# One transfer per convolution row and an earlier reload in a hybrid SSD / S5 / Conformer trunk

## The chip, the cores and the metric

The program runs on one core of one Trainium2 chip. Its time is device time in microseconds (us): 1638.1 us median of 3 runs (1636.99 to 1638.96). The engines are TensorE (PE: matrix products, with a weight load of its own, PEld), VectorE (DVE), ScalarE (ACT), GpSimd (POOL) and SyncE (SP), which here issues nearly all transfers (DMA) from one queue. Each engine runs its instructions in the order in which they stand. PE multiplies 128 x 128 weights with up to 512 columns; its results land in PSUM banks.

## The reference, cut to what matters

512 prompt tokens and 8 x 8 sample tokens (576 columns) of width 1024 pass through two layers. The change is in layer 0:

```python
xn = rms_norm(x)
proj = xn @ w_in_ab                         # z | x,B,C | dt | u
xbc = silu(causal_depthwise_conv(xbc, w=4)) # 2048 channels
cum = cumsum(dt * a)                        # per chunk of 128 tokens, 16 heads
y_diag = (scores * exp(cum_i - cum_j) * dt) @ x      # inside a chunk, causal
y_off  = C @ h_in * exp(cum)                          # from the state before the chunk
h = h * exp(cum_end) + B^T (exp(cum_end - cum) dt x)  # state, chunk to chunk
ya = group_rms_norm((y + d * x) * silu(z))  # 4 groups of 4 heads
yb = s5(u); yb = yb * sigmoid(yb @ w_glu)   # S5 mixer with its GLU
x  = x + concat(ya, yb) @ w_out
```

Then a squared-ReLU MLP; layer 1 is a Conformer convolution module and another MLP; a final norm. Outputs are the activations and the final states of both groups.

## The kernel before

Activations lie with channels on the 128 partitions and the 576 tokens along the row (`NT` = 576, `NP` = 512 prompt tokens, then 64 sample tokens). A product (`mm`, line 232) takes one block of 128 output channels: `load` (line 217) brings 128 x 1024 weights into `raw` (one 512 KB transfer), ACT makes the rounded part `hi`, DVE the rest `lo`, and PE adds hi x act-high, hi x act-low and lo x act-high for 8 blocks of inputs and 2 halves of the tokens: 48 matmuls of 288 columns. Inputs are split in the same way (`split`, `split_scaled`: high part on ACT, low part on DVE).

Layer 0 runs in `mixer0` (line 1061): the S5 input products with the scan, then 24 products of `w_in` (4 groups x [B, C, two of x, two of z]), 8 of `w_glu`, 8 + 8 of `w_out`. Beside them runs the side work of three kinds:
- `s5_y`: eight S5 outputs, the last step of S5; each result `y` goes to a DRAM tensor `yg`.
- `a_conv` (line 767), 16 times, once for each 128 channels of x, B, C. A product's result is copied to `pj` and stored in `prd` (`stash`). `a_conv` loads it to `xb`, multiplies with the norm, does four taps in `cvo` (ACT the first, DVE three 600-wide steps, L784), tanh on ACT (L786), the last step on DVE (L787), and stores to `xsd`. Prompt columns and the 8 x 8 sample columns go in separate transfers, since the sample tokens lie 11 apart in the tile (3 state columns before each 8): L773/L774 load, L788/L789 store. `xb` and `cvo` share one ring of three buffers (tag "cv").
- `a_group` (line 879), four SSD groups, two of them at a time: reload of the rows (`xs`, L889), transposes (`tr`), scores (`scr`), sample state (`h`, `yoff`), then five chunks, each with `sg` (a broadcast load of `cumd`, L943), `yps`, `st` and the state `hst` that goes from chunk to chunk.

`reload` (line 1153) brings the input of the next product back from DRAM: after the input projection `yg` (into `rl`, split to `yh` and `yl`), after the GLU `ybd` (split to `ybh` and `ybl`). The `rl` tiles rotate over three buffers that `pj` uses too.

The order on each engine is set by a scheduler from priorities: code written earlier goes first, and `hp(n)` moves a piece n places ahead. Weights stand 3000 ahead (`HP`), evacuations 149 (`HPE`), the side work 54 (`HPS`); `reload` stands at its place in the code. The side work is called after each product by `side`.

Of the kernel before, what the change touches and what calls it, by code (L numbers as in the profile page):

```python
# [8 lines left out]
F32 = mybir.dt.float32  # L9
F32R = mybir.dt.float32r  # L10
AF = mybir.ActivationFunctionType
ALU = mybir.AluOpType
# [3 lines left out]
NT = 576  # L16
NP = 512
# [121 lines left out]
def h2(t):  # L139
    return t.rearrange("p (h n) -> p h n", h=2)  # L140


class Build:
# [31 lines left out]
    GL = 7  # L175
    X2 = 8
    HPS = 54

    def X(self, name):
        return self.xp.tile([128, NT], F32, tag="X", name=name)  # L180

    def bank(self, name, tag="sd"):
        return self.pd.tile([128, 512], F32, tag=tag, name=name)
# [583 lines left out]
    def a_conv(self, m, rB):  # L767

        nc, q = self.nc, self.q1
        xb = q.tile([128, 603], F32, tag="cv", name="xb", bufs=3)  # L770
        s8 = lambda t, k, n: t[:, 515:603].rearrange("p (b j) -> p b j", b=8)[:, :, k:k + n]
        nc.gpsimd.memset(xb[:, 0:3], 0.0)
        nc.sync.dma_start(xb[:, 3:515], self.prd[m][:, 0:NP])  # L773
        nc.sync.dma_start(s8(xb, 3, 8), self.prd[m][:, NP:].rearrange("p (b j) -> p b j", b=8))  # L774
        nc.scalar.activation(s8(xb, 0, 3), self.aco[:, m, 0:8, :], AF.Copy)
        nc.vector.tensor_tensor(xb[:, 3:515], xb[:, 3:515], rB[:, 0:NP], op=ALU.mult)
        nc.vector.tensor_tensor(s8(xb, 3, 8), s8(xb, 3, 8), rB[:, NP:].rearrange("p (b j) -> p b j", b=8), op=ALU.mult)
        nc.scalar.activation(self.aco[:, m, 8, :], xb[:, 512:515], AF.Copy)
        nc.scalar.activation(self.aco[:, m, 0:8, :], s8(xb, 8, 3), AF.Copy)

        o = q.tile([128, 603], F32, tag="cv", name="cvo", bufs=3)
        nc.scalar.activation(o[:, 0:600], xb[:, 0:600], AF.Identity, scale=self.half("acw", m), bias=self.half("acb", m))  # L782
        for k in range(1, 4):
            nc.vector.scalar_tensor_tensor(o[:, 0:600], xb[:, k:k + 600], self.half("acw", 16 * k + m), o[:, 0:600],  # L784
                                           op0=ALU.mult, op1=ALU.add)
        nc.scalar.activation(xb[:, 0:600], o[:, 0:600], AF.Tanh)  # L786
        nc.vector.scalar_tensor_tensor(o[:, 0:600], xb[:, 0:600], 1.0, o[:, 0:600], op0=ALU.add, op1=ALU.mult)  # L787
        nc.sync.dma_start(self.xsd[m][:, 0:NP], o[:, 0:NP])  # L788
        nc.sync.dma_start(self.xsd[m][:, NP:].rearrange("p (b j) -> p b j", b=8), s8(o, 0, 8))  # L789

    def a_dt_in(self, ps, rB):
        df = self.qs.tile([128, NT], F32, tag="dtf", name="dtf", bufs=1)
        with self.hp(self.HPE):
            self.nc.vector.tensor_tensor(h2(df)[:32], ps[:32], h2(rB)[:32], op=ALU.mult)
        return df

    def a_dt(self, df):

        nc, q = self.nc, self.q1
# [9 lines left out]
        b = self.bank("dtT")  # L809
        for c in range(5):  # L810
            p = 128 if c < 4 else 64
# [3 lines left out]
        for p, c in ((128, slice(0, 4)), (64, slice(4, 5))):  # L815
            k = c.stop - c.start
# [4 lines left out]
        a, e, d, s, z = w(), w(), w(), w(), w()  # L821
# [23 lines left out]
        b = self.bank("cum")  # L845
# [24 lines left out]
        ch = self.qs.tile([128, NT], F32, tag="u3", name="ch", bufs=self.U3)  # L870
        nc.scalar.activation(ch[:16, 0:NP], c0[:16], AF.Copy)
        nc.scalar.activation(ch[:16, NP:], c1[:16, 0:64], AF.Copy)
        nc.sync.dma_start(self.cumd, ch[:16])
        ec = self.u3("ec", NT)
        nc.scalar.activation(ec[:16, 0:NT], ch[:16], AF.Exp)
        nc.sync.dma_start(self.ecd, ec[:16, 0:NT])
# [1 line left out]
    def a_group(self, g, q, X, bank, rB0):  # L878

        nc = self.nc  # L880
        u = str(g % 2)
        k2 = lambda name, *sh: q.tile([128, *sh], F32, tag="sg" + u, name=name, bufs=3)
        k1 = lambda name, *sh: q.tile([128, *sh], F32, tag="k1" + u, name=name, bufs=5)
        hg = slice(4 * g, 4 * g + 4)
        hp = lambda t: t.rearrange("p (h d) -> p h d", h=4)

# [19 lines left out]
        for c in range(5):  # L906
            tok = slice(c * 128, min(c * 128 + 128, NT))
            o = b0[:, tok] if c < 4 else b1[:64, 0:64]
# [12 lines left out]
        b = bank("yoff")  # L921
        for i in range(2):
            h0 = q.tile([128, 4, 256], F32, tag="h0" + u, name="h0", bufs=1)
            nc.sync.dma_start(h0, self.I["ass"][g, :, 4 * i:4 * i + 4, :])
            for j in range(2):
                for s in range(4):
                    t0 = 32 * i + 8 * s
# [5 lines left out]
        for c in range(5):  # L933
            T, t0 = (128, c * 128) if c < 4 else (64, NP)
            tok = slice(t0, t0 + T)
            per = lambda t: t[:T, c, hg].unsqueeze(2).broadcast_to([T, 4, 64])
            xd, xw = k1("xd", 256), k1("xw", 256)
            nc.vector.tensor_tensor(hp(xd[:T]), hp(xt[:T, c]), per(self.dt), op=ALU.mult)
            for e in range(4):
                nc.scalar.activation(xw[:T, e * 64:(e + 1) * 64], xt[:T, c, e * 64:(e + 1) * 64], AF.Copy,  # L940
                                     scale=self.dw[:T, c, 4 * g + e:4 * g + e + 1])
            sg = k2("sg", 4, 128)
            nc.sync.dma_start(sg[:, :, :T], bass.AP(tensor=self.cumd.tensor, offset=self.cumd.offset + 4 * g * NT + t0,  # L943
                                                    ap=[[0, 128], [NT, 4], [1, T]]))
            for e in range(4):

                nc.scalar.activation(sg[:T, e, :T], sg[:T, e, :T], AF.Relu, scale=-1.0, bias=self.cum[:T, c, 4 * g + e:4 * g + e + 1])
            nc.scalar.activation(sg[:T, :, :T], sg[:T, :, :T], AF.Exp, scale=-1.0)
            nc.vector.tensor_tensor(sg[:T, :, :T], sg[:T, :, :T], sc[:T, tok].unsqueeze(1).broadcast_to([T, 4, T]), op=ALU.mult)
            ps = bank("yps")  # L950
            for e in range(4):
                nc.tensor.matmul(ps[64 * (e % 2):64 * (e % 2) + 64, (e // 2) * 128:(e // 2) * 128 + T],  # L952
                                 xd[:T, e * 64:(e + 1) * 64], sg[:T, e, :T], start=True, stop=True)
            if 0 < c < 4:
                t, eb = k1("yt", 2, 128), k1("eb", 2, 128)
                for i in range(2):
                    nc.sync.dma_start(eb[64 * i:64 * i + 64],
                                      bass.AP(tensor=self.ecd.tensor, offset=self.ecd.offset + (4 * g + i) * NT + t0,
                                              ap=[[0, 64], [2 * NT, 2], [1, 128]]))
                for j in range(2):  # L960
                    nc.tensor.matmul(ps[:, 256 + j * 128:384 + j * 128], Hs[:, j * 128:(j + 1) * 128], Cg[:, tok], start=True, stop=True)
                nc.vector.tensor_tensor(t, ps[:, 256:512].rearrange("p (j t) -> p j t", j=2), eb, op=ALU.mult)
                for j in range(2):
                    nc.vector.tensor_tensor(ya[j][:, tok], ps[:, j * 128:(j + 1) * 128], t[:, j], op=ALU.add)
            else:
                for j in range(2):
                    if c < 4:
                        nc.scalar.activation(ya[j][:, tok], ps[:, j * 128:j * 128 + T], AF.Copy)
                    else:
                        nc.vector.tensor_tensor(ya[j][:, tok], ps[:, j * 128:j * 128 + T], yos[:, j], op=ALU.add)  # L970
            if c == 4:
                nc.sync.dma_start(self.btd[g], bt[:64, 4])
                nc.sync.dma_start(self.xwd[g], xw[:64])
            if c < 4:
                b = bank("st")
                nc.tensor.matmul(b[:, 0:256], bt[:, c], xw, start=True, stop=True)
                if c == 0:
                    nc.scalar.activation(Hs, b[:, 0:256], AF.Copy)
                else:
                    nc.vector.tensor_tensor(hp(Hs), hp(Hs), self.cd[:, c, hg].unsqueeze(2).broadcast_to([128, 4, 64]), op=ALU.mult)  # L980
                    nc.vector.tensor_tensor(Hs, Hs, b[:, 0:256], op=ALU.add)
                if c == 3:
                    nc.sync.dma_start(self.O["o_assm"][g, :, 8, :], Hs)
            yield
# [13 lines left out]
        rB = self.bcast_tok(r, "rg", X, bank)  # L998
# [62 lines left out]
    def mixer0(self):  # L1061
        nc, I = self.nc, self.I
        with self.tc.tile_pool(name="q1", bufs=5) as self.q1, ExitStack() as inner:
            self.qs = inner.enter_context(self.tc.tile_pool(name="qs", bufs=2))
            x = []
            for k in range(8):
                t = self.X("xi%d" % k)
# [4 lines left out]
            _, rB = self.rms(x, "rB0")  # L1072
# [6 lines left out]
            for m in range(8):  # L1079
                ps = self.mm(I["w_in"][m], act)  # L1080
                if m < 2:
                    t = self.t("ur", "t")
# [29 lines left out]
            def side(na):  # L1112
# [5 lines left out]
                for _ in range(na):  # L1118
                    with self.hp(self.HPS):
                        if conv:  # L1120
# [33 lines left out]
            def reload(d, f):  # L1154
                out = []
                for k in range(len(d)):
                    t = self.t("rl", "t")
                    nc.sync.dma_start(t, d[k])
                    out.append(f(k, t))
                return out  # L1160

            act = reload(self.yg, lambda k, t: self.split(t, "y", self.B))
# [4 lines left out]
            for m in range(8):  # L1167
                ps = self.mm(I["w_out"][8 + m], act)
                t = self.t("xr", "t")
# [9 lines left out]
            for m in range(8):  # L1179
                t = self.X("x%d" % m)  # L1180
# [249 lines left out]
```

## Time and profile before

| | |
|---|---|
| median of 3 runs | 1638.1 us |
| the profiled execution, its span | 1634.0 us, 1632.2 us |
| PE busy | 1574.1 us (96%) |
| DVE busy, ACT busy | 1056.4 us (65%), 642.3 us (39%) |
| PE's mean granted clock | 0.975 |
| DMA packets, of them under 512 bytes | 185,907, 92,560 |
| mean DMA rate | 135 GB/s |

The profile comes from one execution. "PEclk" or granted clock is the mean share of PE's full clock (2.4 GHz) in a stretch; the lower level is half of it. An idle time is put down to the one that ended it. A transfer "lands" when its data is there and its semaphore is raised. Everything that the change touches stands between 100 and 500 us; the busy times and waits are read in stretches of it below.

### The profile page before, as it was taken

The numbers are of one execution on the slowest core, as the hardware profiler recorded it, in microseconds if no ns is written. First come the engines' busy times: TensorE is split into PE (matmuls) and PEld (weight loads), VectorE is DVE, ScalarE is ACT, GpSimd is POOL, SyncE is SP. The second block draws the span as 40 slices with busy tenths as digits, with TensorE's granted clock in tenths as the row PEclk, the third lists the DMA queues.
The fourth block names the chain that finished last, engine by engine and source line by source line (L and its number), as shares of the span: only waits on it lengthen the run. The fifth ranks groups of instructions, "written<-read, shape, count | busy, mean of one in ns | idle before, by whom it ended". The sixth has DMA issues, their size and how long they took to land.

```text
span 1632.2 us, 28709 instructions
## 1 busy us (share of the span) xinstructions
PE 1574.1 (96%) x11765; PEld 1549.3 (95%) x11765; DVE 1056.4 (65%) x1757; ACT 642.3 (39%) x1084; POOL 4.3 (0%) x42
## 2 busy tenths in 40 slices
PE   7999998989899999999999999997899999999997
PEld 6999998889899999999999999996899999999996
DVE  7968986688865547677744457997554444434466
ACT  4243377775643343332222243332443322222243
POOL 0000000000000000000000000000000000000000
PEclk9999999979899999999999999998899999999998
DMA  5644587988863234454322235541122222222233
GB/s 189 184 120 142 158 226 220 298 251 241 241 229 136 78 96 160 156 135 105 101 79 78 91 133 154 167 136 45 42 88 79 78 91 78 79 90 78 91 118 135
DMA packets 185907, 220.18 MB, mean 135 GB/s; under 512 B 92560, under 2 KB 128400, under 8 KB 185776
## 3 DMA queue, kind: packets, MB, share of 16 engines
q1 hardware_dynamic: 182112, 217.03, 44.3%
q8 instruction: 92, 1.51, 0.4%
q10 hardware_dynamic: 3664, 1.32, 0.3%
q14 instruction: 39, 0.32, 0.1%
HBM read 184.10 MB, written 34.20 MB: 134 GB/s over the span
## 4 chain that ended last, share of the span: by engine, by line
PE 84%; DVE 8%; DMA 5%; issue 1%; ACT 1%; SPq 0%; ACTq 0%; DVEq 0%
PE mm L239 76%; PE pc L1326 2%; DVE acc L1389 1%; DVE lo L225 1%; PE yoff L928 1%; DMA by<-s5bc 1%; PE bc L323 1%; DMA eb<-ecd 1%; DMA xsd<-cvo 1%; PE s5s L613 1%; PE kt L572 1%; PE tsum L293 1%; DVE u L589 1%; PE mu L1301 0%; PE yps L952 0%
## 5 line engine op out<-in xcount | busy, mean ns | idle before, releaser
L224 ACT ACTIVATE hi<-raw 128x1024 fp32r<-128x1024 f32 x217 | 229.7, 1059 | 729.4 <-PE mm L239 633.3
L239 PE MATMUL mm<-fxh,hi 128*128 128x288 f32 x1920 | 417.6, 299 | 14.6 <-ACT hi L224 10.4
L225 DVE TENSOR_TENSOR lo<-raw,hi 128x1024 fp32r<-128x1024 f32 x217 | 264.8, 1221 | 248.0 <-ACT hi L224 243.4
L239 PE MATMUL mm<-fxh,lo 128*128 128x288 f32 x1920 | 415.4, 298 | 0.1
L239 PE MATMUL mm<-fxl,hi 128*128 128x288 f32 x1920 | 414.9, 297 | 0.0
L239 PEld LDWEIGHTS mm<-fxh,hi 128*128 128x128 f32 x1920 | 311.5, 190 | 16.3 <-ACT hi L224 11.3
L239 PEld LDWEIGHTS mm<-fxh,lo 128*128 128x128 f32 x1920 | 311.0, 190 | 1.0 <-DVE lo L225 0.7
L239 PEld LDWEIGHTS mm<-fxl,hi 128*128 128x128 f32 x1920 | 311.1, 190 | 0.5 <-issue 0.2
L239 PE MATMUL mm<-gh,lo 128*128 128x288 f32 x1024 | 229.1, 295 | 1.1 <-DVE lo L225 1.1
L239 PE MATMUL mm<-gh,hi 128*128 128x288 f32 x1024 | 229.6, 295 | 0.0
L239 PE MATMUL mm<-gl,hi 128*128 128x288 f32 x1024 | 229.2, 295 | 0.0
L239 PEld LDWEIGHTS mm<-gh,lo 128*128 128x128 f32 x1024 | 167.9, 188 | 1.5 <-DVE lo L225 1.5
L239 PEld LDWEIGHTS mm<-gl,hi 128*128 128x128 f32 x1024 | 168.3, 188 | 0.0
L239 PEld LDWEIGHTS mm<-gh,hi 128*128 128x128 f32 x1024 | 167.9, 188 | 0.0
L363 DVE TENSOR_TENSOR fft<-mm,r2B 128x576 f32<-128x576 f32 x56 | 42.3, 756 | 116.3 <-PE mm L239 116.3
L1389 DVE SCALAR_TENSOR_TENSOR acc<-hb,vec,acc 128x512 f32<-128x512 f32 x110 | 82.2, 747 | 1.5
L357 DVE TENSOR_TENSOR gl<-ffr,gh 128x576 fp32r<-128x576 f32 x64 | 48.4, 757 | 1.9
L356 DVE TENSOR_TENSOR ffr<-ffr 128x576 f32<-128x576 f32 x64 | 48.5, 757 | 1.6
L355 ACT ACTIVATE gh<-ffr 128x576 fp32r<-128x576 f32 x64 | 43.9, 686 | 2.1
L364 DVE TENSOR_TENSOR x<-x,fft 128x576 f32<-128x576 f32 x56 | 42.3, 756 | 1.6
L784 DVE SCALAR_TENSOR_TENSOR cvo<-xb,vh,cvo 128x600 f32<-128x600 f32 x48 | 40.2, 838 | 1.0 <-ACT cvo L782 0.5
L353 ACT ACTIVATE ffr<-mm 128x576 f32<-128x576 f32 x64 | 40.5, 633 | 0.0
(340 smaller groups left out, 1890.0 us busy)
## 6 DMA issues: line engine op xcount, KB each, us to landing
raw<-w_ff SPq DMA_DIRECT2D x136, 512.0 KB, 3.5
raw<-w_in SPq DMA_DIRECT2D x33, 512.0 KB, 3.8
raw<-w_pw SPq DMA_DIRECT2D x24, 512.0 KB, 3.6
dm<-dwm SPq DMA_DIRECT2D x16, 576.0 KB, 5.6
h<-ass SPq DMA_DIRECT2D x16, 512.0 KB, 4.9
raw<-w_out SPq DMA_DIRECT2D x16, 512.0 KB, 3.6
U<-ud SPq DMA_DIRECT2D x16, 288.0 KB, 4.0
prd<-pj SPq DMA_DIRECT2D x16, 288.0 KB, 2.4
```

The source lines that it names most:

```text
L224: self.last = [nc.sync.dma_start(raw, src), nc.scalar.activation(hi, raw, AF.Copy), eng.tensor_tensor(lo, raw, hi.bitcast(F32), op=ALU.sub ...
L225: eng.tensor_tensor(lo, raw, hi.bitcast(F32), op=ALU.subtract)]
L239: nc.tensor.matmul(ps[:, h, :H], w[:, k], a[:, h * H:(h + 1) * H], start=n == 0, stop=n == 23)
L353: nc.scalar.activation(h2(r), ps, AF.Relu)
L355: nc.scalar.activation(hi, r, AF.Square)
L356: nc.vector.tensor_tensor(r, r, r, op=ALU.mult)
L357: nc.vector.tensor_tensor(lo, r, hi.bitcast(F32), op=ALU.subtract)
L363: nc.vector.tensor_tensor(h2(t), ps, rB, op=ALU.mult)
L364: nc.vector.tensor_tensor(x[m], x[m], t, op=ALU.add)
L784: nc.vector.scalar_tensor_tensor(o[:, 0:600], xb[:, k:k + 600], self.half("acw", 16 * k + m), o[:, 0:600], op0=ALU.mult, op1=ALU.add)
L1326: nc.tensor.matmul(pc[:, g * 128:g * 128 + 128], w[:, j * 128:j * 128 + 128], hq[:, g, j:j + 128], start=j == 0, stop=j == 8)
L1389: nc.vector.scalar_tensor_tensor(ap, hb[:, k:k + NP], w(k), ap, op0=ALU.mult, op1=ALU.add)
```

## The change

1. `a_conv` loads the whole 576-column row into `cvo` with one transfer; the first multiply spreads it into `xb`; the last step is written in two parts into the front of `xb` without gaps, and one transfer stores the row. `xb` and `cvo` have rings of their own with two buffers each.
2. `cumd` is stored chunk by chunk (16 heads x 128 tokens beside each other), so that the load of `sg` reads 2 KB in a row instead of four times 512 bytes.
3. `reload` (load and split) stands 1500 places ahead of its place in the code.
4. To make room, the tile `dtf` shares a ring with `yw`, and the ring "k1" of odd groups has four buffers instead of five.

```diff
+    HPR = 1500
...
     def a_conv(self, m, rB):
         nc, q = self.nc, self.q1
-        xb = q.tile([128, 603], F32, tag="cv", name="xb", bufs=3)
+        o = q.tile([128, 603], F32, tag="co", name="cvo", bufs=2)
+        xb = q.tile([128, 603], F32, tag="cv", name="xb", bufs=2)
         s8 = lambda t, k, n: t[:, 515:603].rearrange("p (b j) -> p b j", b=8)[:, :, k:k + n]
+        c8 = lambda t: t[:, NP:NT].rearrange("p (b j) -> p b j", b=8)
         nc.gpsimd.memset(xb[:, 0:3], 0.0)
-        nc.sync.dma_start(xb[:, 3:515], self.prd[m][:, 0:NP])
-        nc.sync.dma_start(s8(xb, 3, 8), self.prd[m][:, NP:].rearrange("p (b j) -> p b j", b=8))
+        nc.sync.dma_start(o[:, 0:NT], self.prd[m])
         nc.scalar.activation(s8(xb, 0, 3), self.aco[:, m, 0:8, :], AF.Copy)
-        nc.vector.tensor_tensor(xb[:, 3:515], xb[:, 3:515], rB[:, 0:NP], op=ALU.mult)
-        nc.vector.tensor_tensor(s8(xb, 3, 8), s8(xb, 3, 8), rB[:, NP:].rearrange("p (b j) -> p b j", b=8), op=ALU.mult)
+        nc.vector.tensor_tensor(xb[:, 3:515], o[:, 0:NP], rB[:, 0:NP], op=ALU.mult)
+        nc.vector.tensor_tensor(s8(xb, 3, 8), c8(o), c8(rB), op=ALU.mult)
...
-        o = q.tile([128, 603], F32, tag="cv", name="cvo", bufs=3)
         nc.scalar.activation(o[:, 0:600], xb[:, 0:600], AF.Identity, ...)
...
         nc.scalar.activation(xb[:, 0:600], o[:, 0:600], AF.Tanh)
-        nc.vector.scalar_tensor_tensor(o[:, 0:600], xb[:, 0:600], 1.0, o[:, 0:600], op0=ALU.add, op1=ALU.mult)
-        nc.sync.dma_start(self.xsd[m][:, 0:NP], o[:, 0:NP])
-        nc.sync.dma_start(self.xsd[m][:, NP:].rearrange("p (b j) -> p b j", b=8), s8(o, 0, 8))
+        d = xb[:, 0:NT]
+        nc.vector.scalar_tensor_tensor(d[:, 0:NP], xb[:, 0:NP], 1.0, o[:, 0:NP], op0=ALU.add, op1=ALU.mult)
+        nc.vector.scalar_tensor_tensor(c8(d), s8(xb, 0, 8), 1.0, s8(o, 0, 8), op0=ALU.add, op1=ALU.mult)
+        nc.sync.dma_start(self.xsd[m], d)
...
-        df = self.qs.tile([128, NT], F32, tag="dtf", name="dtf", bufs=1)
+        df = self.qs.tile([128, NT], F32, tag="yw", name="dtf", bufs=2)
...
-        nc.sync.dma_start(self.cumd, ch[:16])
+        nc.sync.dma_start(cd(0, (128, 16), (2048, 4), (1, 128)), ch[:16, 0:NP].rearrange("h (c t) -> h c t", c=4))
+        nc.sync.dma_start(cd(16 * NP, (64, 16), (1, 64)), ch[:16, NP:])
...
-        k1 = lambda name, *sh: q.tile([128, *sh], F32, tag="k1" + u, name=name, bufs=5)
+        k1 = lambda name, *sh: q.tile([128, *sh], F32, tag="k1" + u, name=name, bufs=5 - g % 2)
...
-            nc.sync.dma_start(sg[:, :, :T], bass.AP(..., ap=[[0, 128], [NT, 4], [1, T]]))
+            if c < 4:
+                nc.sync.dma_start(sg.rearrange("p h t -> p (h t)"), src([1, 4 * T]))
+            else:
+                nc.sync.dma_start(sg[:, :, :T], src([T, 4], [1, T]))
...
                 for k in range(len(d)):
-                    t = self.t("rl", "t")
-                    nc.sync.dma_start(t, d[k])
-                    out.append(f(k, t))
+                    with self.hp(self.HPR):
+                        t = self.t("rl", "t")
+                        nc.sync.dma_start(t, d[k])
+                        out.append(f(k, t))
```

The scheduler then puts other pieces beside each other. On DVE, in the S5 outputs' stretch of layer 0, the convolutions stood like this before (L776/L777 first multiply, L784 taps, L787 last step; `y`, `yw`, `P` are the S5's):

```order
L733 SCALAR_TENSOR_TENSOR y<-yw,y 128x576
L784 SCALAR_TENSOR_TENSOR cvo<-xb,vh,cvo 128x600
L776 TENSOR_TENSOR xb<-xb,rB_185 128x512
L777 TENSOR_TENSOR xb<-xb,rB_185 128x8x8
L730 TENSOR_SCALAR yw<-yw 128x576
L784 SCALAR_TENSOR_TENSOR cvo<-xb,vh,cvo 128x600
L731 TENSOR_TENSOR yw<-yw,y 128x576
L787 SCALAR_TENSOR_TENSOR cvo<-xb,cvo 128x600
L730 TENSOR_SCALAR yw<-yw 128x576
L733 SCALAR_TENSOR_TENSOR y<-yw,y 128x576
L731 TENSOR_TENSOR yw<-yw,y 128x576
L784 SCALAR_TENSOR_TENSOR cvo<-xb,vh,cvo 128x600 x2
```

After (lines L778/L779, L785, L789/L790):

```order
L778 TENSOR_TENSOR xb<-cvo,rB_185 128x512
L779 TENSOR_TENSOR xb<-cvo,rB_185 128x8x8
L789 SCALAR_TENSOR_TENSOR xb<-xb,cvo 128x512
L790 SCALAR_TENSOR_TENSOR xb<-xb,cvo 128x64
L734 SCALAR_TENSOR_TENSOR y<-yw,y 128x576
L731 TENSOR_SCALAR yw<-yw 128x576
L785 SCALAR_TENSOR_TENSOR cvo<-xb,vh,cvo 128x600
L732 TENSOR_TENSOR yw<-yw,y 128x576
L785 SCALAR_TENSOR_TENSOR cvo<-xb,vh,cvo 128x600
L778 TENSOR_TENSOR xb<-cvo,rB_185 128x512
L779 TENSOR_TENSOR xb<-cvo,rB_185 128x8x8
L785 SCALAR_TENSOR_TENSOR cvo<-xb,vh,cvo 128x600
```

The last step is two instructions now, and the first multiply of the next convolution but one follows it after five other steps.

On SP, at the end of the GLU product (`raw<-w_out` are the next product's weights, `h<-ass` the sample state of the third SSD group), the order was:

```order
L972 DMA btd_413<-bt 64x128
L773 DMA xb<-prd_388 128x512
L774 DMA xb<-prd_388 128x8x8
L224 DMA raw<-w_out 128x1024
L1057 DMA ybd_424<-go 128x576
L1158 DMA rl<-ybd_419 128x576
L788 DMA xsd_381<-cvo 128x512
L789 DMA xsd_381<-cvo 128x8x8
L773 DMA xb<-prd_389 128x512
L774 DMA xb<-prd_389 128x8x8
L924 DMA h_4276<-ass 128x1024
L943 DMA sg<-cumd 128x4x128
```

After:

```order
L964 DMA eb<-ecd 64x2x128 x2
L1166 DMA rl<-ybd_419 128x576
L1064 DMA ybd_424<-go 128x576
L979 DMA btd_413<-bt 64x128
L225 DMA raw<-w_out 128x1024
L1166 DMA rl<-ybd_420 128x576
L1064 DMA ybd_425<-go 128x576
L1166 DMA rl<-ybd_421 128x576
L928 DMA h_4264<-ass 128x1024
L1166 DMA rl<-ybd_422 128x576
L949 DMA sg<-cumd 128x512
```

The loads and stores of the convolutions are gone from here, they stand earlier; three of the reloads `rl<-ybd` now stand ahead of `h<-ass`.

On PE, where the input projection ends (`fxh`) and the GLU product begins (`yh`, `yl`), the order was:

```order
L899 MATMUL tr_3557<-cst,xs_3551 128x128 x4
L900 MATMUL tr_3558<-cst,xs_3551 64x128
L239 MATMUL mm<-fxh,lo 128x288
L952 MATMUL yps<-sg,xd 64x128 x4
L961 MATMUL yps<-xs_3079,hst 128x128 x2
L976 MATMUL st<-xw,bt 128x256
L899 MATMUL tr_3566<-cst,xs_3553 128x128 x4
L900 MATMUL tr_3567<-cst,xs_3553 64x128
L952 MATMUL yps<-sg,xd 64x64 x4
L899 MATMUL tr_3575<-cst,xs_3547 128x128 x4
L900 MATMUL tr_3576<-cst,xs_3547 64x128
L239 MATMUL mm<-yh,hi 128x288 x4
```

After:

```order
L959 MATMUL yps<-sg,xd 64x128 x4
L968 MATMUL yps<-xs_3076,hst 128x128 x2
L983 MATMUL st<-xw,bt 128x256
L903 MATMUL tr_3568<-cst,xs_3540 128x128 x4
L904 MATMUL tr_3569<-cst,xs_3540 64x128
L959 MATMUL yps<-sg,xd 64x128 x4
L968 MATMUL yps<-xs_3076,hst 128x128 x2
L913 MATMUL scr_3578<-xs_3542,xs_3540 128x128 x4
L913 MATMUL scr_3579<-xs_3542,xs_3540 64x64
L983 MATMUL st<-xw,bt 128x256
L240 MATMUL mm<-yh,hi 128x288 x4
L932 MATMUL yoff<-xs_3542,h_3703 128x8 x8
```

A second chunk of the first group (`yps` with `hst`) and the second group's scores (`scr`) stand ahead of the GLU's first matmul; the transposes of the second group (`tr`) stand earlier. The first transposes of the first group stand behind 1322 matmuls of products since the start, before behind 1270.

## Rows read from the trace of the kernel before

**Rows 1.** Busy time by stretch (PE, weight loads, DVE, ACT, POOL), granted clock, DMA share, GB/s

```profile
262.00:271.00 9.00, 6.21 (x29) 6.20 (x30) 5.49 (x9) 4.57 (x9) 0.00 (x0) 0.62 0.90 260
271.00:319.00 48.00, 48.00 (x379) 46.67 (x377) 29.68 (x52) 34.24 (x92) 0.50 (x5) 1.00 1.02 295
319.00:337.00 18.00, 11.66 (x65) 9.72 (x62) 15.55 (x30) 17.02 (x50) 0.10 (x1) 0.72 0.92 254
...
358.00:371.00 13.00, 10.88 (x64) 10.11 (x64) 9.87 (x18) 9.58 (x25) 0.10 (x1) 0.74 0.94 267
...
407.00:422.00 15.00, 12.74 (x77) 12.05 (x76) 11.83 (x19) 9.36 (x22) 0.00 (x0) 0.77 0.97 291
422.00:439.00 17.00, 14.36 (x101) 12.40 (x100) 12.15 (x29) 9.54 (x25) 0.00 (x0) 0.90 0.84 242
...
sum 310.00, PE 291.16 PEld 278.86 DVE 243.48 ACT 196.21 POOL 1.62; mean PE 26.47 PEld 25.35 DVE 22.13 ACT 17.84 POOL 0.15
```

**Rows 2.** PE's waits, 200 to 500 us: total, times, longest

```profile
PE tr L899 <- DMA xs<-xsd: 6.5, 2, 3.4
PE yoff L928 <- DMA h<-ass: 2.3, 1, 2.3
PE mm L239 <- ACT ybh L261: 2.0, 1, 2.0
```

**Rows 3.** Timeline, SP's queue at 256: start, us, line, transfer

```profile
256.12 0.32 SPq L788 DMA_DIRECT2D xsd<-cvo  x1
256.49 0.43 SPq L789 DMA_DIRECT2D xsd<-cvo  x1
261.67 0.32 SPq L889 DMA_DIRECT2D xs<-xsd  x1
```

**Rows 4.** Timeline, PE at two stalls: [idle before it <- releaser]

```profile
264.79 1.08 PE L899 MATMUL tr<-cst,xs 128*128 128x128 f32 x4 [3.41 <-DMA xs<-xsd]
...
330.54 0.85 PE L239 MATMUL mm<-yl,hi 128*128 128x288 f32 x2 [1.52 <-DVE yl L272]
```

**Rows 5.** The chain of waits: two products back to back (start, us)

```profile
615.66 12.80 PE mm L239 x96
```

**Rows 6.** DVE's waits, 230 to 331 us

```profile
DVE xb L776 <- DMA xb<-prd: 12.5, 6, 3.3
DVE cvo L787 <- ACT xb L786: 5.9, 3, 3.7
```

**Rows 7.** Instructions on tile yw, DVE: duration ns min/median/max

```profile
L733 DVE SCALAR_TENSOR_TENSOR y<-yw,y x6: 750/753/759, 224.9 to 258.8; 128x576 f32<-128x576 f32 x6
...
L730 DVE TENSOR_SCALAR yw<-yw x5: 449/454/455, 234.8 to 259.5; 128x576 f32<-128x576 f32 x5
```

**Rows 8.** Instructions on tile xb, DVE, 265 to 300 us

```profile
L784 DVE SCALAR_TENSOR_TENSOR cvo<-xb,vh,cvo x9: 829/843/844, 268.1 to 296.5; 128x600 f32<-128x600 f32 x9
L776 DVE TENSOR_TENSOR xb<-xb,rB x4: 692/694/694, 265.5 to 298.8; 128x512 f32<-128x512 f32 x4
L787 DVE SCALAR_TENSOR_TENSOR cvo<-xb,cvo x4: 776/780/784, 266.1 to 299.5; 128x600 f32<-128x600 f32 x4
L777 DVE TENSOR_TENSOR xb<-xb,rB x4: 207/218/220, 266.8 to 299.4; 128x64 f32<-128x64 f32 x4
```

**Rows 9.** Transfers: count, KB each, median us from issue to landing

```profile
xb<-prd SPq DMA_DIRECT2D x16, 256.0 KB, 3.7
...
xb<-prd SPq DMA_DIRECT2D x16, 32.0 KB, 3.7
```

**Rows 10.** Timeline, SP's queue at 401 to 408

```profile
401.03 2.09 SPq L789 DMA_DIRECT2D xsd<-cvo  x1
406.36 0.32 SPq L773 DMA_DIRECT2D xb<-prd  x1
...
407.26 0.52 SPq L924 DMA_DIRECT2D h<-ass  x1
```

More of the change, by code (lines that the diff above doesn't have):

```diff
@@ L872, in a_dt @@
         nc.scalar.activation(ch[:16, NP:], c1[:16, 0:64], AF.Copy)
-        nc.sync.dma_start(self.cumd, ch[:16])
+        cd = lambda o, *ap: bass.AP(tensor=self.cumd.tensor, offset=self.cumd.offset + o, ap=[list(k) for k in ap])
+        nc.sync.dma_start(cd(0, (128, 16), (2048, 4), (1, 128)), ch[:16, 0:NP].rearrange("h (c t) -> h c t", c=4))
+        nc.sync.dma_start(cd(16 * NP, (64, 16), (1, 64)), ch[:16, NP:])
         ec = self.u3("ec", NT)
@@ L942, in a_group @@
             sg = k2("sg", 4, 128)
-            nc.sync.dma_start(sg[:, :, :T], bass.AP(tensor=self.cumd.tensor, offset=self.cumd.offset + 4 * g * NT + t0,
-                                                    ap=[[0, 128], [NT, 4], [1, T]]))
+            src = lambda *ap: bass.AP(tensor=self.cumd.tensor, offset=self.cumd.offset + 16 * t0 + 4 * g * T, ap=[[0, 128], *ap])
+            if c < 4:
+                nc.sync.dma_start(sg.rearrange("p h t -> p (h t)"), src([1, 4 * T]))
+            else:
+                nc.sync.dma_start(sg[:, :, :T], src([T, 4], [1, T]))
             for e in range(4):
```

## The prediction

> **What bounds the kernel now.** I read three views in this order: busy time by stretch, what TensorE (PE) waited for, and what each releaser had waited for. Outside the stretch from 190 to 500 us the order is nearly the same in both kernels (earlier, only the first convolution loads and the stores of `cumd` differ), so the change has to come from there. In it PE is busy for 291.2 of 310 us [rows 1]: PE is the bound, and what can be won is what PE loses. It loses in two ways. It stands idle (310 - 291.2 = 18.8 us), and after most of the idle spells its granted clock drops from 2.4 to 1.2 GHz. A stretch of T us with mean granted clock g has run 2T(1-g) us at the lower level and lost half of that, T(1-g). From [rows 1], idle plus clock:
> - 262 to 271: 2.8 + 9 x 0.38 = 6.2 us
> - 319 to 337: 6.3 + 18 x 0.28 = 11.4, some 10 when idle time at the lower clock is not counted twice
> - 358 to 371: 2.1 + 13 x 0.26 = 5.5
> - 407 to 422: 2.3 + 15 x 0.23 = 5.7
> - 422 to 439: 2.6 + 17 x 0.10 = 4.3
>
> Between them (271 to 319, 48.0 of 48 at full clock) PE loses nothing. So these five places, 32 us, are all that is worth reading. Their releasers are two reloads of SSD rows (3.4 and 3.1 us), one state tile (2.3) and the split of a reloaded tile (2.0) [rows 2]; behind them stands the convolution `a_conv`.
>
> **Place 1, 262 to 271.** The third convolution's result leaves as two transfers at 256.1 and 256.5; the reload `xs` may go only when both have landed, at 261.7, and PE waits for it until 264.8 [rows 3, 4]. In the new order the first transposes stand 52 product matmuls later (1322 instead of 1270 before them), and 96 take 12.8 us [rows 5], so PE asks 6.9 us later, against 3.4 us of wait. This stall goes.
>
> **Place 2, 319 to 337.** The stall's end is the first `yl` on VectorE (DVE): PE starts the second step of the product at 330.5 when it is there [rows 4]. An earlier PE only waits longer here, so place 1 is no gain by itself; what counts is when DVE reaches `yl`. From 230 to 331 DVE waited 12.5 us in six places for the convolution's input `xb` and 5.9 in three for its tanh [rows 6]. Before, the load of convolution k+2 goes into the tile that the store of k must have left, so two transfers follow each other. After, load and store are both released by the last step of k. DVE then has between that step and the next-but-one's first multiply at least y 0.75, yw 0.45 and 0.75, and two 600-wide steps of 0.84, that is 3.6 us [rows 7, 8], against one landing of 3.7 us at the median [rows 9] and the issue behind the store. I leave 2.0 of the 12.5 us (bounds: 0, and 12.5 if landings stay as long as the two together). Of the tanh waits I take half away (3.0), since two convolutions now interleave; bounds 0 and 5.9.
> Against this stands more work in front of the first `yl` (counted in both orders): six more 600-wide steps (5.0), two more pairs of first multiplies (1.8), two more last steps (1.6), ten last steps split in 512 and 64, each 0.67 + 0.22 - 0.78 = 0.11 dearer (1.1; the 0.67 is an estimate between the 0.69 and the scaled 0.78), one pair of masked scores (0.9), less 3.4 for pieces of the first group that now stand behind: 7.0 us. Net: 7.0 - 10.5 - 3.0 = -6.5 us for places 1 and 2 together.
>
> **Place 3, 358 to 371.** From here DVE has those 7 us behind it. The waits (splits of weights, tanh of the first product) halve: -2.7. Bounds 0 and -5.5.
>
> **Place 4, 407 to 422.** SyncE, which issues every transfer, is done with a store at 403.1 (401.03 + 2.09), then stands until 406.4 because the load `xb` waits for a store to land; the state tile `h` queues behind it and goes at 407.3 [rows 10]. In the new order no convolution load stands in front of this `h`, all 16 are done. It goes some 3 us earlier, more than the 2.3 us that PE waited. But there are 24 instead of 29 product matmuls between the two uses of the tile, 0.7 us less cover. -5.0; bounds 0 and -5.7.
>
> **Place 5, 422 to 439.** Before, three of the eight reloads of `ybd` stand ahead of the last of the stores that fill it, the others come behind it among SSD loads; after, seven of eight do, and their splits stand ahead of the SSD's on ScalarE (ACT) and DVE. The 2.0 us for `ybh` [rows 2] and its clock go in part: -2.8; bounds 0 and -4.3.
>
> **Costs.** DVE gets 16 x 0.11 = 1.8 us more, at places 2 and 3 in DVE's own chain: part of it is in the 7.0, the rest I take as 1. PE meets nine SSD pieces in a row before the first `yh` (six in the old order), with the state of a chunk updated by DVE between them: 1 us. For waits that a new order makes and the old trace cannot show, 2 us, from 0 to 8. Moved loads of weights, `gy` and `xr` keep their places relative to the products that use them: nothing. The one whole `cumd` row per chunk, four times longer pieces for the same bytes, shortens ACT's input and not PE's: nothing; if it does count, it is a gain.
>
> Short pieces: each convolution sent 128 x 8 pieces of 32 bytes twice, 32,768 in all. The 32 KB transfer lands in 3.7 us at the median, the 256 KB beside it in 3.7 too [rows 9]: I give their removal no more than the landings above.
> The Trainium skill (DMA: Bandwidth & Descriptors, Specifications) says that pieces under 512 bytes miss the line rate because they are read, changed and written back. By that rule the queue would be filled by them and the gain would be that of rival B, about 28 us instead of 13; the equal medians do not bear it out, so it gets a small chance.
>
> **Sum.** -6.5 - 2.7 - 5.0 - 2.8 + 1 + 1 + 2 = -13 us. The profiled execution took 1634.0 us (span 1632.2 and 1.8 around it), so 1621 for it. It lies 4.1 below the median of the runs, 1638.1; I forecast the median: **1625 us**.
>
> **Rivals.**
> A. DVE's added work eats what the loads give. For: DVE is busy 15.6 of 18 us at place 2 and 29.7 of 48 before it [rows 1], and 7.0 us more stands before `yl`. If half of the 12.5 us stays as waits and the tanh waits stay, places 1 and 2 give nothing (7.0 - 6.3), and the others half: -5 us, 1633. Against: DVE was idle 18 us before 319.
> B. The short pieces are what fills the queue, which is at 1.02 of its engines in 271 to 319 [rows 1]. Then all landings shorten and all five places go: -32 + 4 of costs = -28, 1610. Against: the equal medians.
> C. Slower. At the change from the input projection to the GLU product two chunks of the first group's state stand bare on PE: `st`, DVE's `hst`, `yps`, again `st`, `hst`, `yps`, with 1.4 to 2.3 us of other pieces between, where before 12 to 24 product matmuls stood between two chunks. If DVE has 3 to 4 us queued before each `hst`, PE idles 8 us more there, and 11.4/6.3 = 1.8 times that with the clock, 14; that takes place 1's 6 us back and, as `yl` and the weights' splits stand behind `hst` on DVE, what places 3 to 5 gave but 2: 14 - 6 - 2 = +6, 1644. It decides from about 3 us of queue per link. Against: the order puts only one split and three short steps between.
> D. Nothing: the reload's priority moves little (its tile rotates over three buffers, so the third waits for the last stash to land anyway), and stalls only change places: 1637.
>
> **How the numbers follow.** Forecast 0.55, its own range 1618 to 1633; A 0.17, B 0.10, C 0.12, D 0.06. A measurement of this kernel tells about 0.2% (3.3 us) from no change. Faster by more: 0.55, B's 0.10 and three quarters of A, 0.78. Within: the rest of A and D, 0.10. Slower: C, 0.12. Range 1610 to 1641, which leaves out half of C and a part of B.
>
> **What would show it.** Right: the first transposes of `xs` without a wait; DVE's wait for `xb` from 230 to 331 at a few us instead of 12.5; the first `yl` near 324; no `yoff` wait of 2 us for `h` at the GLU's end; clock 1.00 around 262 to 271. PE's idle time from 190 to 500 near 10 instead of 18.8 us. Wrong: a wait of PE for `hst` or `yl` of more than 5 us at the change of products (C), DVE still waiting 6 us or more for loads of `prd` (A), or landings of 256 KB under 3 us throughout 271 to 319 (B).

## The result and the profile after

The changed kernel takes 1620.1 us (median of 4 runs, 1615.4 to 1622.5) against 1638.5 for the kernel before: ratio 0.9885, 95% interval 0.9861 to 0.9909. That is 18.5 us less (14.9 to 22.8), where 13 were forecast; the time lies inside the range. The profiled execution has a span of 1617.5 us, 14.7 less than before.

Busy time by stretch after, with the columns of [rows 1]:

```profile
240.00:262.00 22.00, 22.00 (x188) 21.77 (x187) 19.73 (x32) 15.47 (x33) 0.30 (x3) 1.00 0.61 203
262.00:271.00 9.00, 8.59 (x66) 8.35 (x66) 6.50 (x11) 5.51 (x13) 0.10 (x1) 1.00 0.93 311
271.00:319.00 48.00, 44.43 (x335) 42.73 (x335) 35.10 (x62) 36.51 (x94) 0.50 (x5) 0.96 0.92 300
319.00:337.00 18.00, 15.41 (x118) 13.26 (x113) 17.37 (x38) 15.85 (x52) 0.20 (x2) 0.91 0.85 275
337.00:358.00 21.00, 17.19 (x108) 15.40 (x107) 19.14 (x38) 16.59 (x40) 0.10 (x1) 0.84 0.75 251
358.00:371.00 13.00, 12.82 (x97) 12.15 (x97) 10.07 (x24) 6.31 (x17) 0.10 (x1) 1.00 0.85 253
...
407.00:422.00 15.00, 15.00 (x119) 14.03 (x120) 11.22 (x17) 10.35 (x24) 0.00 (x0) 1.00 0.98 330
422.00:439.00 17.00, 17.00 (x135) 15.12 (x134) 13.85 (x33) 10.76 (x32) 0.00 (x0) 0.92 0.58 175
439.00:500.00 61.00, 61.00 (x469) 59.21 (x468) 43.52 (x94) 26.14 (x51) 0.20 (x1) 0.99 0.64 218
```

PE is full, or nearly so, at place 1, at place 3 and from 407 to 500 us. The middle is not better: 271 to 358 held 80.4 us of PE's busy time before (48.00 + 11.66 [rows 1] + 20.72) and 77.0 after. The row of before that [rows 1] leaves out:

```profile
337.00:358.00 21.00, 20.72 (x159) 19.42 (x159) 18.07 (x48) 12.03 (x34) 0.10 (x1) 0.92 0.81 254
```

Over the whole stretch, before and after:

```profile
190.00:500.00 310.00, 291.16 (x2186) 278.86 (x2185) 243.48 (x442) 196.21 (x458) 1.62 (x15) 0.93 0.80 237
```

```profile
190.00:500.00 310.00, 297.83 (x2313) 285.56 (x2313) 254.66 (x470) 199.79 (x464) 1.61 (x15) 0.97 0.76 246
```

PE idles 12.2 us instead of 18.8, and its mean clock rose from 0.93 to 0.97. By the prediction's own reckoning, T(1-g), the clock cost some 22 us before (310 x 0.07) and some 9 after (310 x 0.03; idle time at the lower clock counts in both sums), so more of the gain lies in the clock than in the idle time. What PE still waits for in 200 to 500 us (total, times, longest):

```profile
PE yps L959 <- ACT hst L985: 2.8, 1, 2.8
PE tr L903 <- ACT gs L1060: 1.6, 1, 1.6
PE yps L959 <- DVE xd L942: 1.6, 1, 1.6
PE tr L903 <- DMA xs<-xsd: 1.5, 1, 1.5
PE st L983 <- ACT ya L975: 1.2, 1, 1.2
...
PE tr L903 <- ACT xt L905: 0.9, 1, 0.9
```

Against [rows 2], the waits for `xs` fell from 6.5 to 1.5 us, and those for `h` and `ybh` are no longer there; a link of the state chain (`hst`) has come in.

Where the time went is read best at equal work. Both traces hold all 10,016 product matmuls, so the start of the n-th can be compared, with the count of PE's other instructions (S5, SSD) that stood ahead of it:

| n-th product matmul | before, us | after, us | after - before | less the start's 3.1 | other instructions ahead, after - before |
|---|---|---|---|---|---|
| 1160 | 235.7 | 238.8 | +3.1 | 0 | 0 |
| 1208 | 252.4 | 253.4 | +1.0 | -2.1 | 0 |
| 1304 (place 1) | 272.4 | 266.7 | -5.6 | -8.7 | -5 |
| 1592 (place 2) | 339.0 | 336.7 | -2.3 | -5.4 | +18 |
| 1784 (place 3) | 382.5 | 378.7 | -3.8 | -6.9 | -5 |
| 1976 (place 4) | 428.3 | 416.4 | -11.9 | -15.0 | -33 |
| 2168 (place 5) | 478.6 | 464.7 | -13.9 | -17.0 | 0 |
| 10015, the last | 1618.0 | 1602.8 | -15.2 | -18.3 | 0 |

The 3.1 us at the start arose by 105 us, in S5 code that the change does not touch; in the profiled executions below it is between 0 and 5.1. That of before was at the lower end there, which is probably why the traces differ by less than the medians. The stretch itself gave 17.0 us.

One more row explains most of what follows: the convolutions' stores, with the start of the first and of the last. Before:

```profile
L788 SPq DMA_DIRECT2D xsd<-cvo x16: 314/329/886, 235.0 to 427.0; - x16
```

After:

```profile
L791 SPq DMA_DIRECT2D xsd<-xb x16: 319/320/773, 238.9 to 390.8; - x16
```

The sixteen convolutions took one every 12.8 us before ((427.0 - 235.0) / 15) and take one every 10.1 us now.

### The profile page after: what moved, and what is told of

It reads as the page before. It is cut to its first block, busy times and chain, and to the rows that moved or that the text cites. A ratio compares the mean times of both kernels' runs of the same rounds, so it can differ in the third digit from the quotient of the medians.

```text
span 1617.5 us, 28716 instructions
## 1 busy us (share of the span) xinstructions
PE 1564.0 (97%) x11765; PEld 1540.1 (95%) x11765; DVE 1057.2 (65%) x1773; ACT 641.1 (40%) x1084; POOL 4.3 (0%) x42
## 4 chain that ended last, share of the span: by engine, by line
PE 81%; DVE 7%; DMA 6%; ACT 3%; issue 1%; SPq 1%; ACTq 0%; DVEq 0%
PE mm L240 73%; DVE acc L1397 2%; PE pc L1334 2%; DVE lo L226 1%; DMA xs<-xsd 1%; PE bc L324 1%; DMA rl<-yg 1%; DMA sg<-cumd 1%; DMA cvo<-prd 1%; PE s5s L614 1%; DVE cvo L785 1%; PE s5y L718 1%; PE tsum L1264 1%; PE kt L573 1%; PE s5y L719 1%
## 5 line engine op out<-in xcount | busy, mean ns | idle before, releaser
L240 PE MATMUL mm<-fxh,hi 128*128 128x288 f32 x1920 | 417.2, 299 | 14.9 <-ACT hi L225 10.6
L785 DVE SCALAR_TENSOR_TENSOR cvo<-xb,vh,cvo 128x600 f32<-128x600 f32 x48 | 39.9, 837 | 8.5 <-ACT cvo L783 8.3
```

The costliest lines, as they stand in the source:

```text
L240: nc.tensor.matmul(ps[:, h, :H], w[:, k], a[:, h * H:(h + 1) * H], start=n == 0, stop=n == 23)
```

## The experiments

Theory L: the gain comes from the convolution's load no longer waiting for its own ring's stores. Rivals: R, the reloads that stand earlier; W or P, the whole rows (fewer short packets in a full queue). Ratios are to the kernel before on the same chip. The order is planned anew for each kernel, so each experiment also moves instructions.

**1. Reload alone.** Before, with one edit:

```diff
+                    with self.hp(self.HPR):
                         t = self.t("rl", "t")
```

> The kernel before with one edit, the reloads and their splits 1500 places ahead; the convolution's transfers, rings and cumd as before. Theory L (the gain comes from the convolution's load no longer queueing behind its own store): 1634 to 1638 us, -0 to -4 against before; DVE still waits 10 us or more for xb<-prd from 230 to 331. Theory R (the gain comes from the reloads and splits that stand earlier at the changes of products): 1624 to 1628, -10 to -14, and PE's waits for yh, yl, ybh and for h of the sample state shrink though DVE's waits for prd stay.

Measured: 1635.6 us, ratio 0.9992 (0.9979 to 1.0006): no change that can be told. DVE still waits for the loads from 230 to 331 us, and PE for `h` at the GLU's end (waits of each engine; total, times, longest):

```profile
DVE xb L777 <- DMA xb<-prd: 13.1, 6, 4.0
```

```profile
PE yoff L929 <- DMA h<-ass: 2.8, 1, 2.8
```

SP's queue there (start, us, line, transfer) shows why:

```profile
406.37 1.40 SPq L790 DMA_DIRECT2D xsd<-cvo  x1
411.26 0.32 SPq L774 DMA_DIRECT2D xb<-prd  x1
411.64 0.43 SPq L775 DMA_DIRECT2D xb<-prd  x1
412.16 0.52 SPq L225 DMA_DIRECT2D raw<-w_out  x1
412.78 0.38 SPq L925 DMA_DIRECT2D h<-ass  x1
```

Reloads that stand earlier do not help while a convolution's load stands still in the same queue: SP stands from 407.8 (406.37 + 1.40) to 411.3, and `h` goes only behind that load, as in [rows 10]. Theory R fails as the cause of the whole: alone, this edit saves 3 us at most.

**2. The convolution's edit alone.** `a_conv` as in the change, with the ring changes that make room; `reload` and `cumd` as before.

```diff
+        o = q.tile([128, 603], F32, tag="co", name="cvo", bufs=2)
+        xb = q.tile([128, 603], F32, tag="cv", name="xb", bufs=2)
...
+        nc.sync.dma_start(o[:, 0:NT], self.prd[m])
...
+        nc.sync.dma_start(self.xsd[m], d)
```

> The kernel before with the convolution's edit alone (whole rows, two rings of two buffers, last step in two parts, and the two ring changes that make room); reload and cumd as before. Theory L: 1624 to 1630 us, -8 to -14; DVE's waits for prd from 230 to 331 under 8 us; PE's first transposes without a wait. Theory R: 1634 to 1638, within 4 us of before.

Measured: 1625.5 us, ratio 0.9926 (0.9907 to 0.9945), -12 us. The stores run from 237.4 to 389.7 us, 10.2 us each. DVE's waits for the loads:

```profile
DVE xb L777 <- DMA cvo<-prd: 6.8, 5, 2.9
```

PE meets its first transposes without a listed wait, at 267.4 us. So this edit is two thirds of the gain, as Theory L had it and Theory R had not. It holds both the new rings and the whole rows, so it does not tell L from W; experiment 6 does that in part.

**3. Convolution and reload, `cumd` as before.** The changed kernel with one edit taken back:

```diff
-                nc.sync.dma_start(sg.rearrange("p h t -> p (h t)"), src([1, 4 * T]))
+            nc.sync.dma_start(sg[:, :, :T], bass.AP(..., ap=[[0, 128], [NT, 4], [1, T]]))
```

> The changed kernel with cumd stored and loaded as before (512-byte pieces): all but one edit. If the cumd rows are worth nothing, as the prediction had it: 1618 to 1622, the changed kernel's time. If ACT's waits for sg are behind the bare chain of state tiles: 1624 or more.

Measured: 1619.5 us, ratio 0.9887 (0.987 to 0.9904), the changed kernel's. The one row per chunk is worth nothing. The priority of the reloads, worth at most 3 us by itself (experiment 1), is worth about 6 on top of the new convolution (0.9926 against 0.9887).

**4. Small pieces again.** The changed kernel with the sample columns in a transfer of their own, 32 bytes a piece (the load is shown; the store likewise, and the last step is one instruction again):

```diff
-        nc.sync.dma_start(o[:, 0:NT], self.prd[m])
+        nc.sync.dma_start(o[:, 0:NP], self.prd[m][:, 0:NP])
+        nc.sync.dma_start(s8(o, 3, 8), self.prd[m][:, NP:].rearrange("p (b j) -> p b j", b=8))
```

> The changed kernel, but the convolution's sample columns go in a second transfer of 32-byte pieces again, loads and stores, and the last step is one instruction; the two rings stay. Theory L (the buffers and the order do it): within 4 us of the changed kernel, 1616 to 1624. Theory P (the short pieces filled the queue): 8 us or more is given back, 1628 or more, and landings of the 256 KB rows grow again to 5 us and more beside them.

Measured: 1623.9 us, ratio 0.992 (0.9903 to 0.9937): by the time at the upper end of Theory L's range, by the ratio some 5 us slower than the changed kernel. Most of the gain stays. The 256 KB rows land in 4.5 us at the median (4.6 for the whole rows of the changed kernel), so Theory P's longer landings did not come.

**5. Whole rows, one ring of three.** The changed kernel with

```diff
-        o = q.tile([128, 603], F32, tag="co", name="cvo", bufs=2)
-        xb = q.tile([128, 603], F32, tag="cv", name="xb", bufs=2)
+        o = q.tile([128, 603], F32, tag="cv", name="cvo", bufs=3)
+        xb = q.tile([128, 603], F32, tag="cv", name="xb", bufs=3)
```

> The changed kernel, but xb and cvo share one ring of three buffers again, so that a load must once more wait until the store two convolutions back has landed; whole rows, cumd and the reloads stay. Theory L (the rings' decoupling carries the gain): 8 us or more is given back against the changed kernel, 1628 to 1636. Theory W (whole rows carry it, less time per packet in a queue at its limit): within 4 us of the changed kernel, 1616 to 1624. Half of each: some 1625.

Measured: 1675.7 us, ratio 1.022 (1.0194 to 1.0246): 36 us slower than before. Neither theory had that. The stores:

```profile
L791 SPq DMA_DIRECT2D xsd<-xb x16: 319/323/962, 238.5 to 494.5; - x16
```

17.1 us each. By the ring, a convolution's `xb` takes the buffer of the `cvo` before it, which that one's last step frees: its first multiply must wait for this step, where in the kernel before only ACT's first tap had to. And its `cvo` takes the buffer of an `xb` whose store must have landed. So the convolutions hardly overlap. The table's count shows the result: at product matmul 2216 (469.7 us) 159 of PE's other instructions, of the 1213 done there before and after, are still missing. They are done when few products are left to fill PE. Busy time in 500 to 600 us, in this kernel

```profile
500.00:600.00 100.00, 79.97 (x508) 74.58 (x509) 49.35 (x91) 35.88 (x72) 0.36 (x2) 0.75 0.27 91
```

and in the changed one:

```profile
500.00:600.00 100.00, 100.00 (x756) 99.78 (x755) 50.30 (x71) 37.47 (x51) 0.15 (x1) 1.00 0.27 91
```

20 us idle and a mean clock of 0.75 stand against none. This kernel does more than undo the decoupling, so it shows what the convolutions' pace decides, not the decoupling's share in the 18.5 us.

**6. Rings alone.** Before, with `bufs=4` instead of 3 on "cv" (and the room for it), two transfers, 32-byte pieces.

```diff
-        xb = q.tile([128, 603], F32, tag="cv", name="xb", bufs=3)
+        xb = q.tile([128, 603], F32, tag="cv", name="xb", bufs=4)
```

> The kernel before with four buffers instead of three in the ring that xb and cvo share (so a load no longer waits for a store) and the two ring changes that make room; two transfers with 32-byte pieces, reload and cumd as before. Theory L: 1626 to 1631, most of the 12 us of the convolution's edit alone. Theory W: 1634 to 1638, no more than 3 us.

Measured: 1632.6 us against 1640.3, ratio 0.9956 (0.9938 to 0.9973), -7.2 us by the ratio: short of Theory L's "most of the 12 us", but clear of Theory W's 3. Stores from 236.9 to 407.0, 11.3 us each. The missing wait for the store carries some 7 of the 12 us of experiment 2. The other 5 come with the rest of that edit: whole rows, the split last step, or two rings instead of one. Experiment 4 puts some 5 us on the pieces and the last step, experiment 11 some 6 on the rings; each of these differences is 0.3 to 0.4% with an uncertainty nearly as large, so how the 5 divide is open.

**7. No convolution load.**

```diff
-        nc.sync.dma_start(o[:, 0:NT], self.prd[m])
...
-        nc.vector.tensor_tensor(xb[:, 3:515], o[:, 0:NP], rB[:, 0:NP], op=ALU.mult)
+        nc.vector.tensor_tensor(xb[:, 3:515], rB[:, 0:NP], rB[:, 0:NP], op=ALU.mult)
```

> The changed kernel, but the convolution leaves out its load of prd: its first multiply reads the norm's tile twice. DVE cannot wait for these loads, and 4.7 MB leave the queue. If the 9.1 us that DVE still waits for them from 230 to 331 us bound PE: 1612 or less, 8 us or more under the changed kernel. If PE no longer stands behind them: 1616 to 1622.

Measured: 1617.7 us, ratio 0.9867 (0.9842 to 0.9891), not to be told from the changed kernel. But it does not settle whether DVE's wait binds PE, since another wait took its place, 230 to 331 us:

```profile
DVE xb L777 <- DMA xsd<-xb: 9.5, 3, 6.2
```

The first multiply now waits for the store that must leave `xb`'s buffer, 9.5 us where it waited 9.1 for loads. The last store starts at 390.8 us in both. At equal work its trace is 3.0 us ahead of the changed kernel's (matmul 3000, the start taken off); the timed runs do not resolve that.

**8. Two transfers, 2048 and 256 bytes a partition** (the store likewise).

```diff
+        nc.sync.dma_start(o[:, 0:NP], self.prd[m][:, 0:NP])
+        nc.sync.dma_start(o[:, NP:NT], self.prd[m][:, NP:])
```

> The changed kernel, but the convolution's rows go in two transfers again, of 2048 and 256 bytes a partition, without pieces of 32 bytes; rings, reload and cumd stay. If the size of the pieces made the 5 us between the changed kernel and the one with small pieces: 1617 to 1621, as the changed kernel. If the number of transfers made it: 1623 to 1627.

Measured: 1620.7 us, ratio 0.9894 (0.9871 to 0.9917), as the changed kernel. So the number of transfers costs nothing that can be told. What is left for the 5 us of experiment 4 is the size of the pieces, its last step in one part, or the order planned for them; the difference of the two experiments (0.9894 against 0.9920) is itself no larger than its uncertainty.

**9 and 10. One reload at a time.** The changed kernel with

```diff
-                    with self.hp(self.HPR):
+                    with self.hp(self.HPR if d is self.yg else 0):
```

and, in the other, the reverse (0 for `yg`, `HPR` for the rest).

> The changed kernel with only the first reload (yg, the GLU's input) 1500 places ahead; ybd and yad at their place in the code. If the 6 us that the reloads' priority is worth come from the GLU's end, where the reloads of ybd now go in front of the SSD's loads: 1624 to 1627, as the convolution's edit alone. If they come from the GLU's begin: 1618 to 1622.

> The changed kernel with only the later reloads (ybd, yad) 1500 places ahead, yg at its place in the code. The counterpart: 1618 to 1622 if the GLU's end is where the priority pays, 1624 to 1627 if its begin.

Measured: 1626.1 us, ratio 0.9918 (0.9892 to 0.9945), and 1627.0 us, 0.9923 (0.99 to 0.9946). By the medians both give all of the 6 us back, which the two expectations did not allow together; both intervals still overlap the changed kernel's (0.9861 to 0.9909). At equal work (2216 product matmuls, offset of the start taken off) the first is 2.9 us behind the changed kernel and the second 5.0; the first loses it behind 395 us, where PE waits once more for `h` (0.9 us) and `xs` (1.0), the second from 335 us on, where it waits 1.8 for `yl` and 2.4 for the gate `gs` in front of products (0 and 0.2 in the changed kernel, which waits 1.6 for the gate in front of transposes instead). Both changes of product seem to need it; how the 6 us divide is not settled, since the rest of the timed difference lies behind the stretch, where traces vary by some 4 us.

**11. One ring of four.** The changed kernel with xb and cvo in one ring:

```diff
-        o = q.tile([128, 603], F32, tag="co", name="cvo", bufs=2)
-        xb = q.tile([128, 603], F32, tag="cv", name="xb", bufs=2)
+        o = q.tile([128, 603], F32, tag="cv", name="cvo", bufs=4)
+        xb = q.tile([128, 603], F32, tag="cv", name="xb", bufs=4)
```

> The changed kernel with xb and cvo in one ring of four buffers instead of two rings of two; the same room. A load then still waits only for the last step of the convolution two before, as a ring of four hands each tile its own buffer again. If the number of buffers, and with it the waits, is what counts: 1616 to 1623, as the changed kernel, against 1675.7 with three. If the separate rings matter: 1626 or more.

Measured: 1626.3 us, ratio 0.9926 (0.9904 to 0.9947). By the time just inside the second expectation (1626 or more), yet 49 us better than a ring of three: some 6 worse than two rings. The ring of four has the same two buffers for each tile, but the planned order differs, and the stores end at 405.7 instead of 390.8 us. The number of buffers counts first; the few us left go with the order or with the separate rings, which this run does not tell apart.

**All kernels together.** Product matmul 3000 stands behind the stretch, with the same 1253 other instructions ahead of it in every kernel. Its start, with the offset of the start taken off, against before, goes roughly with the start of the last convolution store. With the last store between 386 and 396 us, 12.3 to 20.4 us are won; with it at 402.8 (experiment 4) 13.0, at 405.7 (11) 10.0, at 407.0 (6) 7.6; at 427.0 (before) and 433.8 (1) nothing; at 494.5 (5) 38.1 us are lost. The kernels differ in more than this pace, so it shows the trend and not the price of one edit.

## Why the prediction was right

- **Whole change.** PE as the bound, the stretch and the sign held: 17.0 us in the stretch at equal work against 13 forecast, and 12.2 us of idle time from 190 to 500 us where "near 10" was expected. That the time came out 5 us below the forecast has its reasons at places 2, 4 and 5 and under the costs.
- **Place 1** went as forecast: the first transposes wait 0.41 us, for another releaser, and the clock is 1.00 where it was 0.62.

```profile
269.72 0.66 PE L903 MATMUL tr<-cst,xs 128*128 128x128 f32 x4 [0.41 <-ACT y L728]
```

- **Place 2 was wrong in its mechanism.** The first `yl` was to come near 324 us, 6.5 earlier. PE meets it at 329.8, with the start's 3.1 us taken off at 326.7, which is 3.8 earlier than the 330.5 of [rows 4]:

```profile
329.80 0.52 PE L240 MATMUL mm<-yl,hi 128*128 128x288 f32 x2
```

 The failed step is "I leave 2.0 of the 12.5 us": DVE still waits 9.1, and where the tanh wait was, ACT's first tap came in (230 to 331 us; the last three rows belong to what follows):

```profile
DVE xb L778 <- DMA cvo<-prd: 9.1, 6, 2.7
DVE cvo L785 <- ACT cvo L783: 5.9, 6, 2.6
DVE lo L226 <- ACT hi L225: 1.6, 2, 1.0
DVE sc L914 <- PE scr L913: 1.2, 2, 0.6
DVE zf L998 <- DMA zf<-zsd: 0.2, 1, 0.2
```

 I had taken the landing as fixed at 3.7 us [rows 9]; it is 4.6 at the median now. The same 288 KB load lands in 3.5 us in experiment 11 and in 5.2 in experiment 5, so it is not the size alone; what else it is stays open. By the sign I had given, more than 6 us of it spoke for rival A, and A's time, 1633, did not come (A's -5 also leaves out the 4 us of costs). What A and I both missed are DVE's other waits in the stretch, which neither sum has. They were 9.3 us before, the rows that [rows 6] leaves out:

```profile
DVE sg L949 <- ACT sg L948: 2.8, 1, 2.8
DVE lo L225 <- ACT hi L224: 2.4, 4, 0.8
DVE yt L962 <- DMA eb<-ecd: 2.1, 1, 2.1
DVE zf L991 <- DMA zf<-zsd: 2.0, 2, 1.6
```

 They are 3.0 after. From 230 us (233.1 after, for the start) to its first `yl`, DVE takes 4.7 us less, and the terms nearly add up to that: 5.8 more work (7.0 forecast), 3.4 less for the loads (10.5), 0.5 less for tanh and first tap (3.0), 6.3 less for the others (nothing). That more pieces were ready for DVE is the likely reason, but no run shows it by itself. So the place came as near to its forecast as it did by a term that was not in the sum, and that is luck.
 By matmul 1592 the two places gave 5.4 us (6.5 forecast): 2.1 before place 1 and 6.6 at it, of which place 2 took 3.3 back. But PE did 23 more of its other instructions between (from -5 to +18 in the table), so the time won at place 1 went into them, and whether "place 1 is no gain by itself" was right cannot be told. In any case this `yl` does not decide the whole: in experiments 6 and 11 it comes 6.3 and 3.5 us later than before, the start taken off, and 7.3 and 9.6 us are won by matmul 2216 all the same.
- **Place 3.** PE idles 0.2 us instead of 2.1, with the clock at 1.00. But `hst` took 2.8 us at 343 and the gate 1.6 at 388: at equal work -1.5 us, -2.7 forecast.
- **Places 4 and 5** gave 10.1 us (from -6.9 to -17.0) where 5.0 + 2.8 = 7.8 were forecast; this term was mis-sized. The state tile `h` goes at 407.0 us, 403.9 with the start taken off, so 3.3 earlier than before (3 forecast), and PE no longer waits for it; experiment 1 shows the same mechanism from the other side. What I had left out is the clock behind the last stall: 439 to 500 us ran at 0.94 before and at 0.99 now, 61 x 0.05 = 3.1 us. I had called the five places "all that is worth reading". The row of this stretch in the kernel before, which I had not weighed:

```profile
439.00:500.00 61.00, 60.90 (x451) 58.06 (x451) 44.08 (x99) 27.41 (x62) 0.21 (x1) 0.94 0.62 209
```

- **Costs.** Of the 4 us, 2 (from 0 to 8) were for waits that a new order makes. Waits of PE that the trace of before does not have, or only as 0.3 us (`hst`), come to some 6.5 us: `hst` 2.8, the gate 1.6, `ya` 1.2, `xt` 0.9. That term was mis-sized within its bounds; what DVE's split last steps cost, no run tells apart. All of it is in the numbers at equal work already. I had priced nothing at 246 us, where PE waited 1.4 us for `y` and no longer does: 2.1 us at matmul 1208, a gain that most of the kernels above show too.
- **Rival B** is right in part. 32-byte pieces are not what made the landings long, which grew without them; but the kernel that has them again loses some 5 us (the pieces, its last step or its order, experiment 8). Busy time in 262 to 337 us of the kernel with small pieces, and behind it of the changed kernel: the DMA engines are busy 0.95 of the time at 277 GB/s with them, 0.90 at 296 without:

```profile
262.00:337.00 75.00, 65.98 (x465) 61.97 (x464) 52.38 (x93) 55.06 (x150) 0.61 (x6) 0.91 0.95 277
```

```profile
262.00:337.00 75.00, 68.43 (x510) 64.34 (x510) 58.97 (x110) 57.88 (x157) 0.80 (x8) 0.95 0.90 296
```

 That is the direction of the Trainium skill (DMA: Bandwidth & Descriptors, Specifications), which puts pieces under 512 bytes below the line rate; the 28 us that rival B drew from it are more than five times too many here.
- **Rival C** came in as one wait of 2.8 us for `hst`, for which the profile names ACT; C had reckoned with 8 us of idle time there, from DVE's queue. **D** fell.
- The 0 for `cumd` held (experiment 3). The reloads' priority, which I had not priced apart, is worth 6 us, and only on top of the other edit.

## What to carry to other kernels

Side work that fills the gaps of a bound engine is judged by its pace: read the first and last start of its stores, divide, and ask whether it ends before the work that hides it. A ring in which a load must wait for a store to land can set that pace, and one buffer more (7 us, experiment 6) was worth more here than a priority alone (3 us at most, experiment 1). The priority paid, 6 us, once no standing transfer was in front of it in its queue. And count a stall with the clock behind it, also in the stretch after the last one.

## What was not expected of the hardware

The sixteen loads of whole rows land no sooner in the changed kernel than the split ones did before [rows 9] (count, KB each, median us to landing):

```profile
cvo<-prd SPq DMA_DIRECT2D x16, 288.0 KB, 4.6
```

Yet the stretch from 262 to 337 us moved more (296 GB/s against 281) at a lower busy share (0.90 against 0.98). And the edit of two tags in experiment 5 took PE's mean granted clock over the whole run from 0.983 to 0.961: with gaps late in the layer, 500 to 540 us went at 0.59, near the lower of its two levels.
